# A Griffin-style hybrid layer on one core: value parts behind the squares, queries in large staging tiles, a cast moved, and a softmax scaling on ScalarE

## The chip, the cores and the metric

The kernel runs on one core of a Trainium2 chip. The metric is the device time of one execution in microseconds (us). Before the change three executions took 1650.82, 1650.87 and 1651.36 us; the median is 1650.87 us. The engines of a core run side by side, each through its own queue in order: TensorE (PE) multiplies and transposes, VectorE (DVE) and ScalarE (ACT) read its results from eight accumulator banks (PSUM), GpSimd (POOL) works on the on-chip buffers alone, and SyncE (SP) issues most of the DMA transfers.

## The reference, cut to what matters

One decoder layer with 1024 tokens of width 1024. The normalised input is projected to the inputs of three branches: a sparse attention (A), a convolution (B) and a cross-attention into 256 memory tokens (C). Gates merge them; an output projection and a gated feed-forward block follow. What the change touches:

```python
# A: queries with 8 heads of 64, keys with 2 groups of 64, both RMS-normalised per head
q = rms_norm(heads(q_nsa, NSA_HEADS), nsa_qk_norm[0])
ks = rms_norm(k_s, nsa_qk_norm[2])      # selected keys; vs = v_s
kw = rms_norm(k_w, nsa_qk_norm[3])      # window keys;   vw = v_w
# B: after the convolution, a layer norm over the channels
u = jax.nn.silu(layer_norm(u, conv_ln_g, conv_ln_b))
# C: four heads of 128 into 256 memory tokens
s_m = jnp.einsum('bshd,bmhd->bhsm', qm, km) * (MEM_HEAD_DIM ** -0.5)
p_m = jax.nn.softmax(s_m, axis=-1)
o_m = jnp.einsum('bhsm,bmhd->bshd', p_m, vm)
```

## The kernel before, in words

**Arithmetic.** Products of 32-bit numbers are made of three products of a rounded high part and the remaining low part. `split` (L130) makes the parts: ACT copies the high part (L131), DVE or POOL subtracts it from the source for the low part (L132). `mm3` (L153, matmuls on L146) multiplies.

**The order of the work.** The Python code issues instructions in a program order. A scheduler then orders each engine's queue at compile time by priority, with modelled durations; a buffer pool gives a tile a buffer when one is free, so too few buffers delay an instruction. `follow` (L207) and the manual dependencies add an order without a wait of their own. On the chip each queue then runs in that fixed order and waits wherever an input or a buffer is not ready. Two kinds of work have low priority and fill gaps: the taps of the convolution on DVE (L474, L475; 120 instructions of about 1000 columns) and the merge-gate products on PE (`pf`, in one bank of their own; ACT empties that bank with the copy L1049).

**Stages around the change.** The mixing projections come first, with the convolution's two operands. Then:

- *Memory attention* (L691, about 245 to 366 us of the profiled execution). Eight units, each two heads by 256 tokens: scores on PE, maxima on DVE (L640), exponentials with their sums on ACT (L644), the reciprocal on DVE (L646), then four multiplications of a 128x256 tile by the reciprocal on POOL (L650). DVE turns the probabilities in squares of 32 (L657), SP stores them (L660) and loads them turned (L665). Two units later `mem_out` makes their parts (ACT cast L670, POOL subtractions L673) and multiplies with the values; its outputs are split again (L684) and stored (L686) for a stage after the attention. Between units, `queries` projects one of eight query tiles (evicted by ACT on L344 and L348), whose raw rows go to memory. From the fourth unit on, `square_queries` (L357) loads such a tile back (L361), scales it on POOL (L363), turns it on DVE (L372) and stores it by four DMAs (L376).
- *Key stage* (L727 to L754, about 343 to 412 us). The weights of 512 columns are loaded in four units, three in the weight buffers and the fourth, as high and low tile, in two of the four large tiles (`t4`, 4 KB a partition). For each of eight token tiles, `wide_proj` makes 24 matmuls into one bank; `heads_norm` (L378) squares the keys on ACT (L382), sums on DVE (L384), takes the root on ACT (L138), the reciprocal (L140) and the product (L387) on DVE. Gains (L745), the split of the keys, and the split of the values straight out of the bank (L749) follow; two tiles later PE transposes the keys (L732) and DVE copies them out (L734). Along with the first four tiles run the query tiles 4 to 7 (raw and turned half in two of six small tiles `t2`), and at tiles 1 and 3 the last two memory outputs. These last query tiles are read only by the second half of the sparse attention.
- *Sparse attention* (412 to about 800 us), and the *merge* (to about 940 us), along with which the layer norm over channels runs in steps (`layer_norm`, L1053): two halves of a mean by a product with ones, two of a variance (L1086), each evicted by a root on ACT (L1088). `bank` (L99) gives out the banks of three pools of 3, 2 and 2 buffers in a fixed rotation; `at` names a pool.

Of the kernel before, what the change touches and what calls it, by code (L numbers as in the profile page):

```python
# [8 lines left out]
F32 = mybir.dt.float32  # L9
# [3 lines left out]
OP = mybir.AluOpType  # L13
# [26 lines left out]
def hybrid_layer_kernel(  # L40
# [48 lines left out]
    def t2(shape, dt=F32, p=P):  # L89
        return t2p.tile([p] + shape, dt, tag="t2", name=nm("t2"))  # L90
# [116 lines left out]
    def follow(m, i, why):  # L207
        tc.add_manual_dep(m.ins, i.name, ORDER, reason=why)
# [145 lines left out]
            follow(m, after, "roots behind the exponentials")  # L354
        nc.vector.reciprocal(stat, stat)

    def square_queries(j, t, stat, after=None):  # L357

        h = stat.shape[2]
        raw, sq = t2([512]), t2([512])  # L360
        nc.sync.dma_start(raw, qraw[j, t])  # L361
        v = raw.rearrange("p (h d) -> p h d", h=h)
        m = nc.gpsimd.tensor_tensor(v, v, stat[:, t, :, None].to_broadcast([P, h, 512 // h]), op=OP.mult)  # L363
        if after is not None:
            follow(m, after, "scaled behind the memory values' parts")
        if j == 0:
            nc.vector.transpose(sq.rearrange("p (c h s) -> p h c s", c=4, h=4),
                                raw.rearrange("p (h c s) -> p h c s", h=4, c=4))
            o = qt_m[t].rearrange("c r a x -> r c a x")
        else:  # L370
            for g in range(2):
                nc.vector.transpose(sq.rearrange("p (g c h s) -> p g h c s", g=2, c=2, h=4)[:, g],  # L372
                                    raw.rearrange("p (g h c s) -> p g h c s", g=2, h=4, c=2)[:, g])
            o = qt_n[t].rearrange("g c r a x -> r (g c) a x")
        for a in range(4):
            nc.sync.dma_start(o[:, :, a], sq[32 * a:32 * a + 32].rearrange("p (c x) -> p c x", c=4))  # L376

    def heads_norm(v, qn):  # L378

        a, h, d = v.shape[1:]  # L380
        sq = t2([a, h, d])
        nc.scalar.activation(sq, v, AF.Square)  # L382
        ss = small(a * h)
        nc.vector.tensor_reduce(ss, sq.rearrange("p a h d -> p (a h) d"), axis=AX.X, op=OP.add)  # L384
        r = recip_rms(ss, d, RMS_EPS, a * h)
        rb = r.rearrange("p (a h) -> p a h", a=a)[:, :, :, None].to_broadcast([P, a, h, d])
        nc.vector.tensor_tensor(qn, v, rb, op=OP.mult)  # L387

    def gain_mul(t, g):
        a, h, d = t.shape[1:]  # L390
# [239 lines left out]
    def mem_softmax(hp, tp, QM):  # L630
        pm = t4([2, 2, 256])
        nb, den, rec = small(4), small(4), small(4)
        bs = []
        for tt in range(2):
            b = bank([2, 256])
            bs.append(b)
            for h in range(2):
                mm3(b[:, h, :], QM[:, 0, tt, h].rearrange("p a s -> p (a s)"), QM[:, 1, tt, h].rearrange("p a s -> p (a s)"),
                    KM[:, 0, 2 * hp + h, :], KM[:, 1, 2 * hp + h, :], True, True)
            nc.vector.tensor_reduce(nb[:, 2 * tt:2 * tt + 2], b, axis=AX.X, op=OP.max, negate=True)  # L640
        for tt in range(2):
            for h in range(2):
                j = 2 * tt + h
                exps.append(nc.scalar.activation(pm[:, tt, h, :], bs[tt][:, h, :], AF.Exp, scale=1.0,  # L644
                                                 bias=nb[:, j:j + 1], accum_out=den[:, j:j + 1]).ins)
        nc.vector.reciprocal(rec, den)  # L646
        for tt in range(2):
            for h in range(2):
                j = 2 * tt + h
                nc.gpsimd.tensor_scalar(pm[:, tt, h, :], pm[:, tt, h, :], rec[:, j:j + 1], 1.0,  # L650
                                        op0=OP.mult, op1=OP.mult)
        return pm

    def mem_squares(hp, tp, pm):
# [11 lines left out]
                          pd[hp, tp].rearrange("m c r a x -> (c r) m (a x)"))  # L666
        return PT

    def mem_out(hp, tp, PT):
        follow(nc.scalar.copy(PT[:, 0], PT[:, 1].bitcast(F32)), exps[-1],  # L670
               "parts behind the next unit's exponentials")
        for mb in range(2):
            part = nc.gpsimd.tensor_tensor(PT[:, 1, mb], PT[:, 1, mb].bitcast(F32), PT[:, 0, mb].bitcast(F32),  # L673
                                           op=OP.subtract)
        o = bank([2, 256])
        for hl, h, mb in [(hl, h, mb) for hl in range(2) for h in range(2) for mb in range(2)]:
            hh = 2 * hp + h
            ov = o[:, h, :].rearrange("p (t a s) -> p t a s", t=2, a=4)
            p_ = PT[:, hl, mb, :, h].rearrange("p a t s -> p t a s")
            mm(ov, VM[:, 0, mb, hh * P:(hh + 1) * P], p_, (hl, h, mb) == (0, 0, 0), (hl, h, mb) == (1, 1, 1))  # L680
            if hl == 0:
                mm(ov, VM[:, 1, mb, hh * P:(hh + 1) * P], p_, False, False)
        om = [PT[:, hl, 0].rearrange("p a h t s -> p (a h t s)").rearrange("p (h t) -> p h t", h=2) for hl in range(2)]
        split(om[0], om[1], o)  # L684
        for hl in range(2):
            follow(nc.sync.dma_start(  # L686
                md[2 * hp:2 * hp + 2, :, hl, tp * 256:(tp + 1) * 256].rearrange("h p t -> p h t"),
                om[hl].bitcast(F32)), stored[-1], "outputs behind the squares")
        return part.ins
# [43 lines left out]
        for s in range(2):  # L733
            nc.vector.tensor_copy(key_cols(s, t), b[:, s].bitcast(F32))  # L734

    cats = []
    for t in range(NT):
        if t < 4:
            square_queries(1, 4 + t, rqn)
        v = wide_proj(ws, t).rearrange("p (s a g d) -> p s a g d", s=2, a=2, g=2)  # L740
        if t in (1, 3):
            mem_out(1, 2 + t // 2, rest.pop(0))
        kn = t2([2, 2, 64])
        heads_norm(v[:, :, 0], kn)
        nc.vector.tensor_tensor(kn, kn, gn[:, 2:4, None, :].to_broadcast([P, 2, 2, 64]), op=OP.mult)  # L745
        cat = t2([4, 2, 64], F32R)
        split(cat[:, :, 0, :], cat[:, :, 1, :], kn.rearrange("p s g d -> p (s g) d"))
        for s in range(2):
            split(VSW[s][:, t, :, 0:64], VSW[s][:, t, :, 64:128], v[:, s, 1])  # L749
        cats.append((t, cat))  # L750
        if t > 1:
            keys(*cats.pop(0))
# [300 lines left out]
    def layer_norm(units):  # L1053
# [27 lines left out]
        yield from sum4(0)  # L1081
        for c in halves:
            yield
            pv = bank([512])
            after = products[-1][0]
            follow(mm(pv, ones, U[0][:, 0, c], True, True), after, "means behind the last products")  # L1086
            rs = t2([512])
            nc.scalar.activation(rs, pv, AF.Sqrt, scale=1.0, bias=LN_EPS)  # L1088
            nc.vector.reciprocal(rs, rs)
            yield  # L1090
            for ct in range(4):
                nc.vector.tensor_tensor(U[ct][:, 1, c], U[ct][:, 1, c], rs, op=OP.mult)
                if ct % 2:
                    yield
# [539 lines left out]
```

## Time and profile before

| | |
|---|---|
| median of three runs | 1650.87 us |
| the profiled execution | 1650.37 us |
| its span (first to last instruction) | 1648.7 us |
| PE idle, 270 to 343 us | 3.85 of 73 us |
| PE idle, 343 to 412 us (key stage) | 7.55 of 69 us |
| PE idle, 412 to 850 us | 2.74 of 438 us |
| L650 on POOL | 32 instructions, 25.6 us |
| L363 on POOL, query tiles of the sparse attention | 8 instructions, 11.1 us |
| L670 on ACT | 8 instructions, 8.5 us |

Times within the execution count from the start of the span. A row such as "L650 POOL TENSOR_SCALAR t<-t,sm 128x256 x32" names the line of the kernel, the engine, the operation, what is written and read by the program's tile names, the shape and the count. Tile names are shared: `ps` are the banks of the three pools, `pf` is the bank of the gate products, `fz` its evicted copy, `t` the large and small tiles, `slab` the large buffers, `wsl` and `fsl` the split weights, `st` and `fst` weights as loaded, `sm` small columns. "A <- B" in the waits means that A stood idle until B was done. PE's busy time counts pipelined matmuls whose ends are modelled.

### The profile page before, as it was taken

The page shows a single profiled execution, that of the slowest core. Times are in us where ns is not written, and L with a number is a line of the kernel's source. Part 1 is how long each engine was busy: PE and PEld are TensorE (multiplying, and loading weights), DVE is VectorE, ACT ScalarE, POOL GpSimd, SP SyncE. Part 2 cuts the span into 40 slices and gives each one's busy share as a digit, 9 for nine tenths or more (in the row PEclk, how much of TensorE's full clock was granted, in tenths as well). Part 3 has the DMA queues.
Part 4 walks back from the last instruction along what each step waited for, and adds up shares of the span by engine and source line. Part 5 has one row for each costly group of instructions (what it writes and reads, how often), then busy time and mean ns, then how long its engine had stood idle before and what let it go on. Part 6 is the DMA issues. An engine that isn't in the chain of part 4 may idle for free.

```text
span 1648.7 us, 22758 instructions
## 1 busy us (share of the span) xinstructions
PE 1622.5 (98%) x7952; PEld 1361.7 (83%) x7952; DVE 1100.8 (67%) x1821; ACT 744.2 (45%) x1370; POOL 678.5 (41%) x567
## 2 busy tenths in 40 slices
PE   8999999989999999999999999999999999999999
PEld 6887898777888888888878889888888888888887
DVE  6389989996565665656686868865454554376665
ACT  6311355432776666665565356532322232233332
POOL 2010005850567757664215441465556677300000
PEclk9999999999999999999999999999999999999999
DMA  8544456753365556347754454333334446893763
GB/s 290 181 156 126 142 155 179 225 177 103 119 177 157 170 147 179 117 137 246 258 196 141 179 167 151 110 109 102 109 103 136 157 142 196 306 372 117 234 233 119
DMA packets 254874, 281.03 MB, mean 170 GB/s; under 512 B 24404, under 2 KB 176260, under 8 KB 253222
## 3 DMA queue, kind: packets, MB, share of 16 engines
q1 hardware_dynamic: 247846, 266.98, 50.7%
q10 hardware_dynamic: 6912, 12.59, 2.0%
q8 instruction: 63, 1.03, 0.3%
q14 instruction: 53, 0.43, 0.1%
HBM read 193.52 MB, written 85.98 MB: 170 GB/s over the span
## 4 chain that ended last, share of the span: by engine, by line
PE 80%; DVE 7%; DMA 4%; issue 3%; POOL 2%; ACT 2%; SPq 1%; ACTq 0%; DVEq 0%; POOLq 0%
PE ps L146 43%; PE pf L146 17%; PE ps L1568 11%; PE ps L1336 3%; DVE slab L475 3%; PE ps L974 2%; PE pf L1568 1%; DMA t<-zd 1%; PE ps L238 1%; DMA t<-qraw 1%; DVE slab L132 1%; DMA st<-in_w_in_dram 1%; POOL slab L1148 1%; PE pf L1336 0%; POOL slab L673 0%
## 5 line engine op out<-in xcount | busy, mean ns | idle before, releaser
L146 PE MATMUL ps<-slab,wsl 128*128 128x512 f32 (+2 forms) x1688 | 362.6, 373 | 0.0
L146 PEld LDWEIGHTS ps<-slab,wsl 128*128 128x128 f32 x1688 | 298.3, 188 | 56.7 <-issue 1.4
L146 PE MATMUL pf<-slab,fsl 128*128 128x512 f32 x1236 | 314.6, 396 | 4.4 <-ACT fz L1049 4.4
L146 PEld LDWEIGHTS pf<-slab,fsl 128*128 128x128 f32 x1236 | 227.6, 189 | 48.9 <-ACT fz L1049 6.0
L475 DVE SCALAR_TENSOR_TENSOR slab<-slab,cw 128x1019 f32<-128x1019 f32 (+16 forms) x120 | 167.2, 1398 | 1.3
L1464 DVE TENSOR_TENSOR t<-ps,t 128x512 f32<-128x512 f32 x130 | 88.9, 688 | 112.0 <-PE ps L146 110.8
L146 PE MATMUL ps<-slab,fsl 128*128 128x512 f32 x684 | 161.9, 391 | 0.5 <-ACT slab L1144 0.5
L146 PE MATMUL ps<-slab,slab 128*128 128x512 f32 (+1 forms) x628 | 151.0, 376 | 2.7 <-POOL slab L673 2.6
L146 PEld LDWEIGHTS ps<-slab,fsl 128*128 128x128 f32 x684 | 127.7, 188 | 28.0 <-issue 0.7
L146 PEld LDWEIGHTS ps<-slab,slab 128*128 128x128 f32 x628 | 112.8, 188 | 25.6 <-POOL slab L673 4.2
L1568 PE MATMUL ps<-wsl 128*128 128x512 f32 x495 | 118.9, 389 | 0.0
L1568 PEld LDWEIGHTS ps<-wsl 128*128 128x128 f32 x495 | 92.9, 188 | 19.3
L132 DVE TENSOR_TENSOR wsl<-st,wsl 128x1024 fp32r<-128x1024 f32 x58 | 81.3, 1404 | 29.5 <-ACT wsl L131 27.1
L146 PE MATMUL ps<-wsl,slab 128*128 128x512 f32 (+1 forms) x480 | 96.0, 349 | 2.3 <-DVE wsl L132 1.8
L131 ACT CAST wsl<-st 128x1024 fp32r<-128x1024 f32 x61 | 63.8, 1051 | 71.1 <-PE ps L146 23.9
L146 PE MATMUL ps<-slab,qt 128*128 128x384 f32 (+6 forms) x400 | 93.3, 336 | 0.7 <-DVE sm L837 0.3
L132 DVE TENSOR_TENSOR t<-ps,t 128x512 fp32r<-128x512 f32 (+2 forms) x96 | 61.2, 641 | 40.6 <-ACT t L131 39.7
L146 PEld LDWEIGHTS ps<-wsl,slab 128*128 128x128 f32 x480 | 76.7, 189 | 13.2 <-DVE wsl L132 2.0
L146 PE MATMUL ps<-t,slab 128*128 128x256 f32 (+1 forms) x404 | 86.7, 318 | 0.0
L131 ACT CAST wsl<-t 128x1024 fp32r<-128x1024 f32 x43 | 45.3, 1053 | 87.0 <-POOL t L128 32.7
L1477 POOL TENSOR_TENSOR t<-t,t 128x512 f32<-128x512 f32 x21 | 39.3, 1872 | 109.6 <-DVE t L1464 43.4
L1148 POOL TENSOR_TENSOR slab<-slab,t 128x512 f32<-128x512 f32 x32 | 47.8, 1514 | 81.6 <-DVE t L1147 81.6
(267 smaller groups left out, 2964.2 us busy)
## 6 DMA issues: line engine op xcount, KB each, us to landing
t<-in_w_down_dram SPq DMA_DIRECT2D x70, 256.0 KB, 3.7
fst<-in_w_in_dram SPq DMA_DIRECT2D x24, 512.0 KB, 4.0
zd<-fz ACTq DMA_DIRECT2D x48, 256.0 KB, 2.7
slab<-wd SPq DMA_DIRECT2D x24, 512.0 KB, 4.6
t<-zd SPq DMA_DIRECT2D x24, 512.0 KB, 3.9
st<-in_w_gate_dram SPq DMA_DIRECT2D x22, 512.0 KB, 4.0
st<-in_w_up_dram SPq DMA_DIRECT2D x22, 512.0 KB, 4.2
ad<-t SPq DMA_DIRECT2D x44, 256.0 KB, 2.8
```

The lines of the kernel that those rows point to most:

```text
L131: m = nc.scalar.copy(hi, src)
L132: return m, (eng or nc.vector).tensor_tensor(lo, src, hi.bitcast(F32), op=OP.subtract)
L146: m = nc.tensor.matmul(o, a, b, start=start, stop=stop)
L238: m = nc.tensor.transpose(b[:, kk, tt * P:(tt + 1) * P], js[tt][:, k * P:(k + 1) * P], ident)
L475: return nc.vector.scalar_tensor_tensor(acc[:, s:], u[:, :S - s], cw[:, ct, 30 - s:31 - s], acc[:, s:], op0=OP.mult, op1=OP.add)
L974: nc.tensor.transpose(b[:, j - j0, h, :], tiles[h][:, j * P:(j + 1) * P], ident)
L1148: nc.gpsimd.tensor_tensor(a, a, z, op=OP.add)
L1336: nc.tensor.matmul(B[j], a_(ha, k, j), w[:, hb, k % 2, :], start=start and k == 0 and n_ == 0, stop=stop and k == 3 and n_ == 2, skip_grou ...
L1464: nc.vector.tensor_tensor(o, a_, b_, op=OP.add)
L1477: nc.gpsimd.tensor_tensor(u4, u4, c22, op=OP.mult)
L1568: nc.tensor.matmul(B[t], a_, b_, start=start and k == 0 and j == 0, stop=k == FH - 1 and j == 2, skip_group_check=True)
```

## The change

Five edits:

- `square_fetch` is new and only loads a query tile. In the key stage the tiles 4 and 5 are fetched ahead of the loop, 6 and 7 behind the first two uses, each into one large tile whose halves hold the raw and the turned rows.
- `heads_norm` takes two callbacks. In the key stage the high parts of the values (two ACT copies) come directly behind the squares, and the low parts (two DVE subtractions) directly behind the sum, in place of the split at the end of a tile's work. It returns the squares' instruction.
- The last memory output's cast (`mem_out` at tile 3) is ordered behind the squares of key tile 1 and not behind the last exponential.
- The four multiplications of a memory unit by the reciprocals go from POOL to ACT, as copies with a scale.
- The second variance product of the layer norm takes its bank from the first pool; the rotation moves on as before.

```diff
-    def square_queries(j, t, stat, after=None):
+    def square_fetch(j, t, bufs):
+        nc.sync.dma_start(bufs[0], qraw[j, t])
+        return bufs
+
+    def square_queries(j, t, stat, after=None, bufs=None):
 
         h = stat.shape[2]
-        raw, sq = t2([512]), t2([512])
-        nc.sync.dma_start(raw, qraw[j, t])
+        raw, sq = bufs or square_fetch(j, t, (t2([512]), t2([512])))
...
-    def heads_norm(v, qn):
+    def heads_norm(v, qn, highs=None, others=None):
 
         a, h, d = v.shape[1:]
         sq = t2([a, h, d])
-        nc.scalar.activation(sq, v, AF.Square)
+        m = nc.scalar.activation(sq, v, AF.Square)
+        if highs:
+            highs()
         ss = small(a * h)
         nc.vector.tensor_reduce(ss, sq.rearrange("p a h d -> p (a h) d"), axis=AX.X, op=OP.add)
+        if others:
+            others()
         r = recip_rms(ss, d, RMS_EPS, a * h)
         rb = r.rearrange("p (a h) -> p a h", a=a)[:, :, :, None].to_broadcast([P, a, h, d])
         nc.vector.tensor_tensor(qn, v, rb, op=OP.mult)
+        return m.ins
...
-                nc.gpsimd.tensor_scalar(pm[:, tt, h, :], pm[:, tt, h, :], rec[:, j:j + 1], 1.0,
-                                        op0=OP.mult, op1=OP.mult)
+                nc.scalar.activation(pm[:, tt, h, :], pm[:, tt, h, :], AF.Copy, scale=rec[:, j:j + 1])
...
-    def mem_out(hp, tp, PT):
-        follow(nc.scalar.copy(PT[:, 0], PT[:, 1].bitcast(F32)), exps[-1],
+    def mem_out(hp, tp, PT, after=None):
+        follow(nc.scalar.copy(PT[:, 0], PT[:, 1].bitcast(F32)), after or exps[-1],
                "parts behind the next unit's exponentials")
...
-    cats = []
+    def fetch(t):
+        r = t4([2, 512])
+        return square_fetch(1, t, (r[:, 0], r[:, 1]))
+
+    cats, fetched, kept = [], [fetch(4), fetch(5)], []
     for t in range(NT):
         if t < 4:
-            square_queries(1, 4 + t, rqn)
+            square_queries(1, 4 + t, rqn, bufs=fetched.pop(0))
+            if t < 2:
+                fetched.append(fetch(6 + t))
         v = wide_proj(ws, t).rearrange("p (s a g d) -> p s a g d", s=2, a=2, g=2)
         if t in (1, 3):
-            mem_out(1, 2 + t // 2, rest.pop(0))
+            mem_out(1, 2 + t // 2, rest.pop(0), kept[t - 2] if t == 3 else None)
         kn = t2([2, 2, 64])
-        heads_norm(v[:, :, 0], kn)
+        vh, vl = ([VSW[s][:, t, :, 64 * l:64 * l + 64] for s in range(2)] for l in range(2))
+
+        def highs():
+            for s in range(2):
+                nc.scalar.copy(vh[s], v[:, s, 1])
+
+        def others():
+            for s in range(2):
+                sub(nc.vector, vl[s], v[:, s, 1], vh[s].bitcast(F32))
+
+        kept.append(heads_norm(v[:, :, 0], kn, highs, others))
         nc.vector.tensor_tensor(kn, kn, gn[:, 2:4, None, :].to_broadcast([P, 2, 2, 64]), op=OP.mult)
         cat = t2([4, 2, 64], F32R)
         split(cat[:, :, 0, :], cat[:, :, 1, :], kn.rearrange("p s g d -> p (s g) d"))
-        for s in range(2):
-            split(VSW[s][:, t, :, 0:64], VSW[s][:, t, :, 64:128], v[:, s, 1])
         cats.append((t, cat))
...
+            turn[1] += c is halves[1]
-            pv = bank([512])
+            pv = bank([512], at=0 if c is halves[1] else None)
             after = products[-1][0]
```

## The prediction

> **What bounds the kernel now.** I read the page first, then the busy times by stage, then who makes TensorE (PE) wait, and last the chain of work inside the stage that the change edits.
>
> ```profile
> span 1648.7 us, 22758 instructions
> PE 1622.5 (98%) x7952; PEld 1361.7 (83%) x7952; DVE 1100.8 (67%) x1821; ACT 744.2 (45%) x1370; POOL 678.5 (41%) x567
> ```
>
> PE is busy 1622.5 of 1648.7 us. The change adds no matmul and takes none away, so whatever it is worth lies in the 26 us in which PE stands still, or runs slowly. The busy times by stage say where those are (columns: window, its length, then busy time and count for PE, PEld, DVE, ACT and POOL, the granted clock, DMA share, GB/s).
>
> ```profile
> 270.00:343.00 73.00, 69.15 (x356) 57.41 (x355) 71.06 (x78) 39.84 (x94) 54.59 (x47) 1.00 0.77 226
> 343.00:412.00 69.00, 61.45 (x289) 50.46 (x288) 52.14 (x105) 17.85 (x51) 15.92 (x12) 0.98 0.38 116
> 412.00:850.00 438.00, 435.26 (x2323) 371.31 (x2322) 271.80 (x826) 289.31 (x651) 250.95 (x258) 1.00 0.56 175
> ```
>
> The end of the memory attention (270 to 343) leaves PE idle for 3.9 us, the key stage (343 to 412) for 7.5 us, and the whole attention behind it, 438 us long, for 2.7 us. In the first DVE is full (71.06 of 73 us, with the convolution taps of L475 as its cheap filling); in the second nothing is full, so its idle time is waiting. Who is waited for:
>
> ```profile
> PE pf L146 <- ACT fz L1049: 4.4, 5, 2.9
> PE ps L146 <- POOL slab L673: 2.6, 3, 1.3
> PE ps L732 <- DVE t L132: 2.0, 1, 2.0
> PE ps L146 <- DVE wsl L132: 1.8, 1, 1.8
> PE ps L146 <- ACT t L131: 1.2, 2, 1.0
> PE ps L146 <- ACT t L1088: 0.5, 1, 0.5
> ```
>
> The columns are total, times, longest. The 2.9 us, the 2.0 us and the 1.8 us are single events of the key stage. The chain of waits shows the first:
>
> ```profile
> 384.32 2.77 DMA t<-qraw
> 387.25 1.05 POOL t L363
> 388.33 0.77 DVE t L372 x2
> 389.10 0.31 DVE sm L384
> 389.43 0.21 ACT sm L138
> 389.64 0.48 ACT fz L1049
> 390.17 6.48 PE pf L146 x21
> ```
>
> A query tile that only the later attention needs is loaded (L361), scaled on POOL (L363) and turned on DVE (L372). DVE runs its queue in order, so the key statistics (L384) stand behind L372; ACT's root (L138) stands behind those; and the copy L1049, which empties the one bank of the gate products, stands behind the root. PE, which would have filled its time with gate products, waits for that bank. The load came so late because it stood on SP behind the previous tile's stores (L376). The second wait has a chain too:
>
> ```profile
> 359.93 1.05 ACT slab L670
> 360.98 0.29 ACT t L382
> 361.30 0.42 DVE sm L384
> 361.71 1.70 DVE slab L475
> 365.54 0.41 DVE t L387
> 365.95 1.62 DVE slab L475
> 367.57 0.33 DVE t L745
> 368.11 1.16 DVE slab L475
> 369.27 0.07 DVE t L132
> ```
>
> ACT held the squares of the first key tile (L382) behind the last memory cast (L670), which was waiting for its load; then each DVE step of the tile's normalisation stood behind a tap.
>
> **The 2.9 us cost more than themselves.** The same windows around that gap:
>
> ```profile
> 387.20:390.10 2.90, 0.07 (x1) 0.00 (x0) 1.47 (x5) 0.67 (x3) 1.04 (x1) 0.95 0.03 9
> 390.10:393.30 3.20, 3.13 (x8) 2.50 (x9) 3.17 (x8) 1.98 (x6) 0.00 (x0) 0.51 0.51 155
> ```
>
> Behind the gap PE was granted 0.51 of its clock for 3.2 us: 3.2 x (1 - 0.51) = 1.6 us of work lost. A 2.9 us gap is enough for that here. The Trainium skill ("TensorE: Matmul & The Clock Gate", Part 1) puts the fall to half clock after an idle window of about 3.4 us and gives as a rule that no gap may pass that; by it this gap would not be charged, and the sum below would be 5.2 us and not 6.8, the time 1645.7. The row decides, and gives that no chance: the clock did fall.
>
> **The change, part by part.**
>
> *Queries in large tiles.* The loads of query tiles 4 and 5 leave SP at the start of the key stage, those of 6 and 7 after tiles 4 and 5, each into a buffer of the four-buffer pool of large tiles (4 KB a partition, raw half and turned half) and no longer into two of the six small ones. The number of loads, scalings, turns and stores is the same; four issues move ahead of stores on SP.
>
> ```profile
> L361 SPq DMA_DIRECT2D t<-qraw x16: 323/455/1117, 88.0 to 384.3; - x16
> ```
>
> At 455 ns each (median) that is 1.8 us of SP earlier and 1.8 us less later, net nothing. DVE then finds L372's input there, L384 is not held, L1049 comes at once: the 2.9 us and the 1.6 us of half clock go. This I count in full, 4.5 us. Only if the tiles are not free in time does it not come (a rival below). What is late next on that place is the copy of the single gate bank itself, a fraction of a microsecond.
>
> *Last cast later.* L670 of the last memory unit is now ordered behind the squares of the second key tile. The first tile's squares then don't wait for a load. The cast (1.05 us), its two subtractions (L673), the 12 products and the stores behind them come later; nobody reads these stores before the end of the attention, hundreds of microseconds on, so the delay costs nothing. The chain above then starts earlier by at least the cast's own 1.05 us.
>
> *Value parts directly behind squares.* In the trace:
>
> ```profile
> ACT slab L131 <- DVE t L387: 11.6, 7, 4.0
> ```
>
> The value casts wait for L387, because one bank's readers are kept in program order across engines. Now the two casts follow the squares on ACT, and the two subtractions run on DVE between the sum and the reciprocal, while ACT takes the root. A bank is free after L387 and not after four more steps. The key chain gets two short casts (128x128; less than the 0.41 us below) before the root and two subtractions before L140, at most 0.8 us on each engine, and about 0 where ACT and DVE wait for each other anyway. With the earlier start, of the 2.0 us wait at L732 I take 1.5 as gained; the ends are 2.0 gained, and 1.8 lost (next to the taps, below).
>
> *Scaling on ACT.* POOL's 32 multiplications become 32 ACT copies with a scale.
>
> ```profile
> L650 POOL TENSOR_SCALAR t<-t,sm 128x256 f32<-128x256 f32 x32 | 25.6, 816 | 1.2 <-DVE sm L646 1.2
> L650 POOL TENSOR_SCALAR t<-t,sm x32: 472/482/2478, 251.8 to 349.9; 128x256 f32<-128x256 f32 x32
> L131 ACT CAST t<-t 128x256 fp32r<-128x256 f32 x10 | 3.6, 414 | 0.0
> ```
>
> POOL loses 25.6 us; ACT gains some 32 x 0.414 = 13.2 us (the nearest row, the same shape between buffers) in a stretch where it was busy 39.84 of 73 us. A unit's four take 1.7 us in place of 3.3, and the subtractions L673 and L132 no longer stand behind them on POOL. Of the 2.6 us that PE waits for L673 I take 0.8 as gained (ends: 0, if it is the casts L670 ahead of POOL that are late, and 2.6). DVE gains hardly anything:
>
> ```profile
> 343.61 2.02 DVE L475 SCALAR_TENSOR_TENSOR slab<-slab,cw 128x1008 f32<-128x1008 f32 x1
> 347.26 1.24 DVE L475 SCALAR_TENSOR_TENSOR slab<-slab,cw 128x1007 f32<-128x1007 f32 x1
> 344.53 2.00 POOL L363 TENSOR_TENSOR t<-t,spent 128x512 f32<-128x512 f32 x1
> 346.52 3.84 POOL L650 TENSOR_SCALAR t<-t,sm 128x256 f32<-128x256 f32 x4
> ```
>
> A tap beside POOL's L363 takes 2.02 us, one beside L650 takes 1.24: it is L650 that gets stretched (482 ns median, 2478 longest), not the tap. The Trainium skill ("SBUF — State Buffer", SBUF: two separate sides) calls the port pair of DVE and POOL an exclusive lock, held for a whole instruction; by it each L650 could hold off a tap for its 0.48 us, 32 x 0.48 = 15 us of DVE freed as an estimate from the row. The two taps speak against any such size, so I count 0; the case in which it comes is a rival.
>
> The cost is ACT's order. The four copies wait for the reciprocal L646, and that stands among the taps:
>
> ```profile
> 335.24 0.20 ACT L644 ACTIVATION_READ_ACCUMULATOR t<-ps,sm 128x1 f32 x1
> 341.12 0.17 DVE L646 RECIPROCAL sm<-sm 128x4 f32<-128x4 f32 x1
> ```
>
> In the last unit 5.7 us lie between the last exponential and its reciprocal. POOL could wait that long at no cost; ACT has behind it the copies that empty PE's banks (L344, L1049) and weight casts. The cost lies between 0 (the compile-time order puts these ahead of the scaling) and 5.7 us plus a half clock for a unit like the last. I take 1.0 in all: most of what ACT does then does not feed PE at once.
>
> *Layer norm bank.* The second variance product takes a bank of the first pool; the 0.5 us wait for L1088 should go: 0.5.
>
> *Key weights.* The 1.8 us wait for the weights' subtraction (DVE wsl L132) is not edited. POOL and DVE arrive a little earlier; I take 0.5 (ends 0 and 1.8).
>
> **The sum.** 2.9 + 1.6 + 1.5 + 0.8 + 0.5 + 0.5 - 1.0 = 6.8 us. The profiled execution took 1650.37 us (its span 1648.7 and 1.7 around it) and lies 0.5 us under the median 1650.87: 1650.87 - 6.8 = 1644.1 us.
>
> **The rivals.**
>
> *Everything relaxes.* With POOL freed, and DVE too, the memory stage's waits go (L673 1.8 more, the casts' 1.2), the weights' 1.3 more, L732's last 0.5, and ACT costs nothing (1.0): 6.8 + 5.8 = 12.6, 1638.3 us. For it speaks DVE at 71.06 of 73 us; against it the tap that took 1.24 us. (The lock that the Trainium skill describes in "SBUF — State Buffer" would be a way to it.) Chance 0.14.
>
> *The taps take the stage back.* PE arrives earlier at the key transposes, by the 4.5 us, but each step of the chain still stands behind a tap (1.70, 1.62 and 1.16 us above). Then L732's wait is not 0.5 but 2.0 + 1.8, and weights and POOL give nothing: 6.8 - 3.3 - 0.5 - 0.8 = 2.2, 1648.7 us. For it: taps are not touched. Against: they sit early in the stage. Chance 0.14.
>
> *The change does not do what it says.* The large pool's four buffers also hold the last memory unit and the last quarter of the key weights. If the fetches wait for these, tiles 6 and 7 arrive late again and 4.5 us stay: 1648.6 us. Against it: two buffers free themselves before the stage needs them, and query tile 6 is used two key tiles later. Chance 0.08.
>
> *Slower: ACT is blocked by the scaling.* Place: the eight units of the memory attention. If two of them stall PE as long as the last reciprocal lags, each also falls to half clock: 2 x (5.7 + 1.6) = 14.6, less the 7.8 of the gains: 1657.7 us. It decides against the change from 11.1 us of stalls on (7.8 + 3.3). Against it: ACT was idle for 33 of 73 us. Chance 0.08.
>
> **How the numbers follow.** The forecast gets 0.56. A difference of 0.2% (3.3 us) is about what a measurement of this kernel can tell from no change, so faster means under 1647.6. Forecast and first rival lie there: 0.70; the two that end at 1648.7 make no change: 0.22; slower 0.08. The range runs from 1639.0, just above the first rival, to 1650.5, above both of the unchanged ones; it leaves out the slower case and the tail of the first rival. The likeliest case alone spans 1641.5 to 1647.
>
> **What would show it.** Right: in the changed profile no PE wait for L1049 over 1 us between 343 and 412, no stretch there at a clock of 0.5, no DVE wait of L372 for L363, L382 of the first key tile no longer behind L670, L650 on ACT at about 0.41 us each, and no wait for L1088. The memory stage's idle 3.9 us should shrink slightly and the attention's 2.7 us stay. Wrong: a wait of PE for ACT between 270 and 343 that was not there, a half clock anywhere new, or L732's wait grown. If the key stage loses its 4.5 us and the time still stays, the static order of the fillers gave it back after 412.

## The result and the profile after

The changed kernel takes 1642.59 us (median of four runs, 1641.7 to 1643.48), the kernel before beside it 1651.11 us (1650.82 to 1653.25): a ratio of 0.9948, 95% interval 0.9937 to 0.9960, 8.5 us less. The forecast was 1644.1 us and 6.8 us less. The sum is near; what stands in it is not, as the profile after and twelve more kernels show.

The page of the profiled execution (1642.26 us) begins:

```profile
span 1640.2 us, 22729 instructions
PE 1621.2 (99%) x7952; PEld 1363.5 (83%) x7952; DVE 1095.1 (67%) x1821; ACT 756.0 (46%) x1402; POOL 658.3 (40%) x535
```

POOL is 20 us less busy and ACT 12 us more. By stages, the columns as before:

```profile
270.00:343.00 73.00, 71.54 (x380) 61.16 (x379) 72.01 (x85) 52.37 (x122) 46.66 (x28) 1.00 0.81 243
343.00:412.00 69.00, 64.10 (x295) 52.47 (x294) 47.15 (x107) 16.34 (x50) 10.33 (x8) 0.95 0.30 95
412.00:850.00 438.00, 436.40 (x2320) 371.87 (x2319) 275.44 (x819) 290.21 (x650) 249.74 (x257) 1.00 0.56 175
```

Read the counts before the busy time. In the 73 us of the memory stage PE began 380 matmuls, not 356. Its busy time rose by only 2.4 us, but 24 matmuls at 71.54 / 380 = 0.188 us are 4.5 us of work; by their shapes, twelve of 512 columns at 0.227 us and twelve of 256 at 0.118 us (median distance between two starts), 4.1 us. So busy time also holds some longer distances between matmuls. In the key stage PE is idle for 4.9 us in place of 7.5, but its mean clock fell from 0.98 to 0.95. From 412 to 850 the idle time fell from 2.7 to 1.6 us. One stretch further on, before and then after:

```profile
850.00:1060.00 210.00, 209.17 (x1041) 176.47 (x1040) 162.89 (x198) 108.25 (x163) 82.69 (x51) 1.00 0.44 147
```

```profile
850.00:1060.00 210.00, 210.00 (x1050) 178.53 (x1049) 162.44 (x200) 106.93 (x162) 92.18 (x55) 1.00 0.45 151
```

The last 0.8 us of idle time are gone there. By these counts the changed kernel is 24 matmuls ahead at 343 us, 30 at 412 us, 27 at 850 us and 36 at 1060 us. Who PE waits for, in the changed kernel (fz L1049 has become L1070, POOL L673 is L680, L732 is L739, the last cast L670 is L677; a wait of 6.0 us near the start, 5.9 before, is left out):

```profile
...
PE ps L146 <- ACT slab L677: 3.4, 1, 3.4
PE pf L146 <- ACT fz L1070: 1.0, 3, 0.4
PE ps L146 <- DVE t L132: 1.0, 2, 0.6
PE ps L146 <- POOL slab L680: 0.8, 2, 0.4
...
PE ps L739 <- DVE t L132: 0.5, 1, 0.5
```

The single 2.9 us for fz and the 1.8 us for the key weights are gone, and the 2.0 us at the key transposes have become 0.5. In their place stands a wait that was not there, 3.4 us for the last memory cast, at 359.2 us. The windows around it:

```profile
359.20:362.60 3.40, 0.01 (x1) 0.00 (x0) 2.47 (x5) 1.95 (x5) 1.29 (x1) 1.00 0.39 116
362.60:369.50 6.90, 6.38 (x21) 5.10 (x22) 6.90 (x12) 0.68 (x2) 3.33 (x2) 0.53 0.24 76
```

Behind it PE has 0.53 of its clock for 6.9 us: 6.9 x 0.47 = 3.2 us lost, twice the 1.6 us of before. So the wait and the half clock behind it cost 6.6 us, where the fz gap and its half clock had cost 4.5. What PE waited for is in DVE's queue:

```profile
350.16 0.77 DVE L375 STREAM_TRANSPOSE t<-t 128x256 f32<-128x256 f32 x2 [2.94 <-POOL t L366]
350.85 1.40 DVE L483 SCALAR_TENSOR_TENSOR slab<-slab,cw 128x1005 f32<-128x1005 f32 x1
352.18 0.76 DVE L375 STREAM_TRANSPOSE t<-t 128x256 f32<-128x256 f32 x2
352.86 1.22 DVE L483 SCALAR_TENSOR_TENSOR slab<-slab,cw 128x1004 f32<-128x1004 f32 x1
354.00 0.41 DVE L389 TENSOR_REDUCE sm<-t 128x4 f32<-128x256 f32 x1
...
360.17 0.42 DVE L768 TENSOR_TENSOR t<-t,spent 128x256 f32<-128x256 f32 x1
```

and in ACT's:

```profile
360.63 0.41 ACT L131 CAST t<-t 128x256 fp32r<-128x256 f32 x1 [5.98 <-DVE t L768]
360.94 0.38 ACT L385 ACTIVATE t<-ps 128x256 f32<-128x256 f32 x1
361.21 0.42 ACT L761 CAST slab<-ps 128x128 fp32r<-128x128 f32 x2
361.51 1.07 ACT L677 CAST slab<-slab 128x1024 fp32r<-128x1024 f32 x1
```

DVE stands 2.94 us before the turn of a query tile (L375), whose rows have just been fetched and scaled. Behind it come a tap, a second query tile, a tap, and only then the sum of the first key tile (L389, 354.00). The root on ACT follows, then reciprocal, product and gains on DVE, each of these three behind a tap and the last also behind the turns of a third query tile (358.34). Then ACT can cast that tile's keys (360.63), and the squares of the second tile and the last memory cast, which the change put behind those squares, follow. PE had finished the products of four key tiles and the fillers that fit by 359.2.

The first row maximum of the sparse attention (one row of the trace, first and last start; before, then after) tells how far ahead the kernel is:

```profile
L848 DVE DVE_READ_ACCUMULATOR2_ANT sm<- x208: 73/83/85, 417.0 to 779.8; 128x1 f32 x104
```

```profile
L869 DVE DVE_READ_ACCUMULATOR2_ANT sm<- x208: 72/83/89, 411.1 to 773.1; 128x1 f32 x104
```

It begins 5.9 us earlier and ends 6.7 us earlier, and the span is 8.5 us shorter. Two thirds of the lead in matmuls (24 of 36) are there before the key stage begins. Does it come from the scaling, or from the key stage's edits, as the prediction's terms have it?

### The profile page after: what moved, and what is told of

Same layout as the page of the kernel before. It is cut to its first block, busy times and chain, and to the rows that moved or that the text cites. A ratio compares the mean times of both kernels' runs of the same rounds, so it can differ in the third digit from the quotient of the medians.

```text
span 1640.2 us, 22729 instructions
## 1 busy us (share of the span) xinstructions
PE 1621.2 (99%) x7952; PEld 1363.5 (83%) x7952; DVE 1095.1 (67%) x1821; ACT 756.0 (46%) x1402; POOL 658.3 (40%) x535
## 4 chain that ended last, share of the span: by engine, by line
PE 83%; DVE 8%; POOL 2%; DMA 2%; issue 2%; ACT 1%; SPq 1%; ACTq 0%; DVEq 0%; POOLq 0%
PE ps L146 47%; PE pf L146 16%; PE ps L1590 11%; PE ps L1358 4%; DVE slab L483 4%; PE ps L995 2%; PE pf L1590 1%; PE ps L238 1%; DMA t<-qraw 1%; PE pf L1358 1%; POOL slab L797 1%; POOL slab L132 0%; POOL wsl L797 0%; DVE wsl L132 0%; SPq L379 0%
## 5 line engine op out<-in xcount | busy, mean ns | idle before, releaser
L483 DVE SCALAR_TENSOR_TENSOR slab<-slab,cw 128x1019 f32<-128x1019 f32 (+16 forms) x120 | 160.4, 1341 | 1.3
L131 ACT CAST wsl<-st 128x1024 fp32r<-128x1024 f32 x61 | 63.9, 1052 | 72.0 <-PE ps L146 24.6
L131 ACT CAST wsl<-t 128x1024 fp32r<-128x1024 f32 x43 | 45.3, 1053 | 87.9 <-POOL t L128 33.5
```

Of the source, the lines that this page charges most:

```text
L131: m = nc.scalar.copy(hi, src)
L483: return nc.vector.scalar_tensor_tensor(acc[:, s:], u[:, :S - s], cw[:, ct, 30 - s:31 - s], acc[:, s:], op0=OP.mult, op1=OP.add)
```

## The experiments

My theory after the first look gave the scaling 2.4 us, the fall of the memory stage's idle time from 3.85 to 1.46 us. The rival gave it nothing and the whole gain to the key stage, as the prediction had. Each kernel was timed beside the kernel before (medians 1651.76, 1650.70 and 1650.97 us in the three sessions). The ratios are estimated over the single executions and not from the two medians; they differ by up to 0.001 from the medians' quotient.

| kernel | median us | ratio to before | 95% interval |
|---|---|---|---|
| u_scale: change, scaling back on POOL | 1649.0 | 0.9989 | 0.9980 to 0.9998 |
| o_scale: before, scaling on ACT alone | 1641.82 | 0.9949 | 0.9936 to 0.9961 |
| o_scale_pool: the same, POOL loaded again | 1645.13 | 0.9962 | 0.9949 to 0.9976 |
| o_dve: before, scaling on DVE | 1651.87 | 1.0003 | 0.9994 to 1.0012 |
| u_cast: change, last cast ordered as before | 1642.56 | 0.9948 | 0.9936 to 0.9961 |
| u_values: change, values split at the end | 1643.79 | 0.9961 | 0.9949 to 0.9974 |
| u_tiles: change, queries in small tiles | 1639.38 | 0.9926 | 0.9913 to 0.9939 |
| c_prod_late: change, last memory products later | 1641.88 | 0.9944 | 0.9930 to 0.9957 |
| q_later: change, query tiles two key tiles later | 1641.93 | 0.9946 | 0.9933 to 0.9958 |
| q_follow: q_later, turns behind the first keys | 1634.58 | 0.9900 | 0.9884 to 0.9916 |
| c_taps: change without the last 14 taps (its output lacks them) | 1641.28 | 0.9940 | 0.9926 to 0.9953 |
| o_scale_qfollow: o_scale, turns behind the first keys | 1641.17 | 0.9936 | 0.9923 to 0.9949 |

### Which half of the change brings the time

u_scale is the change without the edit of the scaling, o_scale that edit alone.

```diff
# u_scale, on the changed kernel
-                nc.scalar.activation(pm[:, tt, h, :], pm[:, tt, h, :], AF.Copy, scale=rec[:, j:j + 1])
+                nc.gpsimd.tensor_scalar(pm[:, tt, h, :], pm[:, tt, h, :], rec[:, j:j + 1], 1.0, op0=OP.mult, op1=OP.mult)
# o_scale, on the kernel before: the same two lines the other way round, and nothing else
```

> The change with the four multiplications of a memory unit back on POOL, all else as changed. Theory A (the scaling on ACT is what took PE's idle time between 270 and 343 us from 3.85 to 1.46 us): about 2.4 us slower than the change, 1645 us, with the idle time of that stage back near 3.9 us. Rival B (the whole gain is made in the key stage; the scaling only moves work between engines): within 1 us of the change, 1642.6 us.

> The kernel before with the scaling on ACT alone. Theory A: the memory stage's idle time falls by some 2.4 us and the key stage keeps its 7.5 us: 1648.5 us. Rival B: 1651 us, no change. Rival C (ACT blocked by the reciprocal's wait): slower than 1652 us, with PE waits for ACT between 250 and 343 us.

All forecasts missed both kernels: u_scale is 4 us slower than the slower one had it, and o_scale 6.7 us faster than the fastest. o_scale alone is as fast as the whole change (0.9949 and 0.9948); everything but the scaling is worth 1.8 us (u_scale, 0.9989, interval 0.9980 to 0.9998). The prediction had given the scaling 0.8 - 1.0 = -0.2 us, and the key stage's edits 6.0. In u_scale PE's waits of the key stage are no smaller than before:

```profile
PE ps L146 <- ACT slab L678: 4.2, 1, 4.2
PE ps L146 <- DVE wsl L132: 2.7, 1, 2.7
```

### Why the scaling is worth it

Two mechanisms were open: POOL's queue is freed (its subtractions come earlier), or the softmax chain is shorter on ACT. o_scale_pool loads POOL with a multiplication of the same shape for every copy, whose result nobody reads; o_dve frees POOL without touching ACT.

```diff
# o_scale_pool, on o_scale
                 nc.scalar.activation(pm[:, tt, h, :], pm[:, tt, h, :], AF.Copy, scale=rec[:, j:j + 1])
+                nc.gpsimd.tensor_scalar(spent[:, 256:512], spent[:, 0:256], rec[:, j:j + 1], 1.0,
+                                        op0=OP.mult, op1=OP.mult)
# o_dve, on the kernel before
-                nc.gpsimd.tensor_scalar(pm[:, tt, h, :], pm[:, tt, h, :], rec[:, j:j + 1], 1.0,
+                nc.vector.tensor_scalar(pm[:, tt, h, :], pm[:, tt, h, :], rec[:, j:j + 1], 1.0,
```

> The kernel before with the scaling on ACT, and beside each of the 32 copies a POOL multiplication of the same shape that also waits for the reciprocal and writes into constants no longer in use, so that POOL keeps the 25.6 us that it was rid of. Theory A (the gain of the scaling is POOL's queue: its parts for L132 and L673 stand no longer behind the scaling): most of the 9 us goes again, 1648 to 1650 us. Rival B (the gain is the shorter chain from exponentials to turned squares, four scalings in 1.7 us for 3.3): the gain stays, 1642 to 1644 us. Rival C (DVE gains, because POOL takes less of the port pair that they share): the taps' mean, 1.40 us before, stays there and the gain goes as under A.

> The kernel before with the four multiplications on DVE in place of POOL, and nothing on ACT. Theory A (POOL's queue): POOL is rid of them, most of the gain comes, less what DVE, which is full there, pays for 32 more instructions: 1643 to 1647 us. Rival B (the shorter chain): DVE does them in its own queue right before it turns the squares, the chain is as short: also 1643 to 1647 us. Rival C (DVE's time is what bounds the memory stage): 32 more instructions of about 0.3 us make it slower than ACT's by 10 us: 1651 us or more.

The whole memory stage (245 to 343 us), in the order before, o_scale, o_scale_pool, o_dve:

```profile
245.00:343.00 98.00, 94.15 (x494) 79.23 (x493) 94.68 (x103) 50.68 (x122) 65.96 (x59) 1.00 0.71 209
```

```profile
245.00:343.00 98.00, 96.36 (x518) 82.92 (x517) 94.56 (x111) 66.83 (x159) 52.07 (x32) 1.00 0.75 227
```

```profile
245.00:343.00 98.00, 94.27 (x500) 80.36 (x500) 92.22 (x103) 62.38 (x152) 69.38 (x58) 1.00 0.70 210
```

```profile
245.00:343.00 98.00, 93.49 (x486) 79.61 (x486) 97.84 (x125) 46.97 (x117) 37.14 (x27) 0.98 0.64 189
```

How long ACT waits there for the score maxima on DVE (total, times, longest), in the same order:

```profile
ACT t L644 <- DVE sm L640: 29.5, 11, 6.6
```

```profile
ACT t L644 <- DVE sm L640: 9.5, 7, 3.3
```

```profile
ACT t L644 <- DVE sm L640: 9.9, 5, 3.8
```

```profile
ACT t L644 <- DVE sm L640: 24.5, 10, 6.4
```

And the taps there, before and in o_scale:

```profile
L475 DVE SCALAR_TENSOR_TENSOR slab<-slab,cw 128x1013 f32<-128x1013 f32 (+29 forms) x35 | 55.2, 1581 | 0.1
```

```profile
L475 DVE SCALAR_TENSOR_TENSOR slab<-slab,cw 128x1013 f32<-128x1013 f32 (+29 forms) x36 | 50.9, 1417 | 0.1
```

With the scaling on ACT, DVE does the same taps in less time (mean 1581 to 1417 ns, 36 x 0.164 = 5.9 us of a full engine), the maxima come earlier, and PE fits 24 more matmuls into the same 98 us. Loading POOL again (69.38 us busy) leaves ACT's wait short (9.9 us), but takes 18 of the 24 matmuls back, and 2 us of the time by the ratios (3.3 us by the medians); the two intervals overlap. The time, 1645.13 us, lies between what the queue alone (1648 to 1650) and the shorter chain alone (1642 to 1644) would give. So more than half of the gain (6.3 of 8.4 us by the ratios) is there with POOL as loaded as before, and part of it may be POOL's queue: the matmuls say so, the times do not tell it apart from nothing. Freeing POOL at DVE's expense brings nothing at all: DVE is busy for 97.84 of 98 us. My expectation for o_dve had the multiplication's cost on DVE wrong:

```profile
L650 DVE TENSOR_SCALAR t<-t,sm x28: 341/824/1390, 251.7 to 336.3; 128x256 f32<-128x256 f32 x28
```

Its median in this stage is 824 ns (584 ns over all 32), where 300 had been assumed.

POOL's total load does not order the taps: they took 1474 ns on the mean in o_scale_pool, with POOL at its fullest. What POOL does meanwhile does, when the 35 taps that begin between 245 and 343 us are sorted by it (from the traces' starts and ends; POOL's are rough). In the kernel before, 8 taps beside no POOL instruction took 1.25 us on the mean, 3 beside multiplications alone 1.33, and 18 beside two-input instructions alone (the subtractions and L363) 1.78, the longest 2.32. In o_scale_pool these means are 1.26 (7 taps), 1.37 (9) and 1.67 (15). So a tap is long mainly beside a two-input instruction, and hardly beside a multiplication. In o_scale 24 taps ran beside two-input instructions, at 1.51 us; why they are stretched less there is not shown. Nor do shorter taps alone explain the short wait of ACT: in o_dve they took 1357 ns, the least of the four, and the wait is 24.5 us.

### The key stage's edits one by one

```diff
# u_cast, on the changed kernel
-            mem_out(1, 2 + t // 2, rest.pop(0), kept[t - 2] if t == 3 else None)
+            mem_out(1, 2 + t // 2, rest.pop(0))
# u_values
-        kept.append(heads_norm(v[:, :, 0], kn, highs, others))
+        kept.append(heads_norm(v[:, :, 0], kn))
...
+        for s in range(2):
+            split(VSW[s][:, t, :, 0:64], VSW[s][:, t, :, 64:128], v[:, s, 1])
# u_tiles
-            square_queries(1, 4 + t, rqn, bufs=fetched.pop(0))
-            if t < 2:
-                fetched.append(fetch(6 + t))
+            square_queries(1, 4 + t, rqn)
```

> The change with the last memory cast ordered behind the last exponential again, as before. Theory A (the new order is itself what PE waits for: a gap of 3.4 us for the cast L677, and behind it 6.8 us at half clock, another 3.4 us): the gap goes, about 5 us faster than the change, 1637.5 us. Rival B (the gap comes from the query loads that hold DVE up, and the new order spares the first tile's squares a wait): 1 to 3 us slower than the change, 1644 to 1645.5 us.

> The change with the values split at the end of a tile's work again, as before. Theory A (the new order frees a bank some steps earlier, but the first tile's chain behind DVE's queue is what is late): within 1 us of the change, 1642.6 us. Rival B (the earlier free bank is worth the 1.5 us that the prediction gave it with the cast): 1644 us or more.

> The change without its large staging tiles: the queries are fetched at each key tile's turn into small tiles again. If the early fetches are worth nothing (theory: VectorE waited for the fetched rows in the changed kernel too, 4.6 us against 6.5 before), this is within 1.5 us of the change, ratio 0.994 to 0.9955, with the gap of 3 to 4 us before 365 us still there. If the prediction's step was right (the large tiles bring the rows early enough to shorten the first tile's chain), the gap and the half clock behind it grow and it is 2.5 us or more slower than the change, ratio over 0.996.

The place of the last cast is worth nothing (0.9948 twice), which neither forecast had: with the old order the cast is done early, and the same gap ends at the key transposes instead (3.5 us). The value parts may be worth 1 to 2 us (0.9961, intervals overlapping); their profiled execution also had half clock in stages that the edit does not touch, so I read no more from it. The large tiles look like a loss (the intervals only touch, at 0.9937 to 0.9939), and the trace shows why. Without them PE's wait before the first key transposes is

```profile
PE ps L739 <- DVE t L132: 1.9, 1, 1.9
```

in place of 3.4 us, the key stage's clock 0.98 in place of 0.95, and the time 3.2 us less. Both theories had it no faster than the change. The early fetches did bring the rows earlier, for two tiles at once, and so in the changed kernel the turns of all four tiles stand ahead of the first key tile's last subtraction (363.36). With small tiles only the first query tile's do (351.21). The first sum comes no earlier there (354.35, behind a second tap in place of the second tile), but the steps behind it are not held, and the last subtraction is at 361.01.

### What makes the gap of 3.4 us

Three answers: the order on PE (the last memory products are planned too early), the turns of the query tiles ahead of the first key sum, or the taps between the steps of the first key chain.

```diff
# c_prod_late, on the changed kernel: in mem_out, for the last memory output; behind = the last key product of tile 3
+            m = mm(ov, VM[:, 0, mb, hh * P:(hh + 1) * P], p_, (hl, h, mb) == (0, 0, 0), (hl, h, mb) == (1, 1, 1))
+            if behind is not None:
+                follow(m, behind, "outputs behind the last key products")
# q_later, on the changed kernel
-        if t < 4:
-            square_queries(1, 4 + t, rqn, bufs=fetched.pop(0))
-            if t < 2:
-                fetched.append(fetch(6 + t))
+        if 2 <= t < 6:
+            square_queries(1, 2 + t, rqn, bufs=fetched.pop(0))
+            if t < 4:
+                fetched.append(fetch(4 + t))
# q_follow, on q_later: for each of a query tile's turns
+                if behind is not None:
+                    follow(m, behind, "turned behind the first keys")
# with behind = the last subtraction of the first key tile's split
# c_taps, on the changed kernel; NOUT = 14
-            while j < len(taps) and run * (len(taps) + TAP_LEAD) >= j * total:
+            while j < len(taps) - NOUT and run * (len(taps) + TAP_LEAD) >= j * total:
# o_scale_qfollow: o_scale with the edits of q_later (small tiles) and q_follow
```

> The change, and the products of the last memory output ordered on PE behind the key products of tile 3. Theory A (PE stands at the cast only because its queue has these 12 products too early): the 3.4 us gap and the 3.4 us lost to half clock go, 1636 to 1637 us. Rival B (what is late is the DVE work that waits for query loads; PE would stand at the key transposes in place of the products): 1641.5 to 1643 us.

> The change with the query tiles 4 to 7 handled at key tiles 2 to 5 and not 0 to 3. Theory A (PE's 3.4 us gap in the key stage comes from DVE, whose queue holds the first key tile's sum, L389, behind query transposes that wait for POOL and for the late loads): the gap and the half clock behind it go, some 5 to 6 us, 1637 us. Rival B (the taps between the steps of that chain are enough to keep it late): the gap stays at 2 us or more, 1640.5 to 1643 us.

Both times lie where the rivals put them, but not for the rivals' reasons. The products that c_prod_late was to hold back stood behind the key tiles' products already, and its wait is 3.8 us for the same cast. q_later moved the query tiles in the program, but that only changes a priority: the scheduler gave the turns the same place on DVE, at 350.07 us with a wait of 3.18. So neither tested what it was to test.

> The change, with the turns of the fetched queries (VectorE, two instructions of 0.77 us a tile) put behind the first key tile's last subtraction; nothing else is moved. In the changed kernel VectorE stood 2.94 us before these turns, for the fetched rows, and the first tile's sum came behind two tiles of them, at 354.00 us. Theory (the gap of 3.4 us of TensorE at 362 us is the length of the first key tile's chain on VectorE): the sum now comes at about 350 us, the chain ends about 5 us earlier, the gap is under 0.7 us and the granted clock stays full between 343 and 412 us: 5 to 7 us less than the change, about 1636 us, ratio 0.991. Rival (the taps between the steps, or ScalarE's queue, hold the chain; the turns only fill a hole): a gap of 2 us or more stays, with half clock behind it, and the time is within 1.5 us of the change (0.9945 to 0.995).

> The change without the last 14 taps of the convolution (of 124; its output lacks them): those that VectorE did between 344 and 375 us as filler between the steps of the first key tiles. The turns of the fetched queries stay ahead of the first sum. Theory (length of the first tile's chain): the sum waits for the turns as before, until about 351.7 us, but the five taps behind it (5 x 1.25 = 6.2 us) are gone from the chain: gap under 0.7 us, full clock, 5 to 7 us less than the change, ratio about 0.991. Rival (the wait for the fetched rows alone holds the chain, taps only fill holes): the gap stays at 2 us or more and the time within 1.5 us of the change. If both this kernel and the one with the turns behind lose the gap, neither alone is its cause: the sum of both is.

> The kernel before with two edits alone: the scaling of the memory probabilities on ScalarE, and the query turns behind the first key tile's last subtraction (their place in the program two tiles later). No split of the value parts, no large tiles, no bank of its own. Theory (the change's own key edits are worth nothing, the turns are what holds the key stage): as fast as the change with the turns behind, about 1636 us, ratio 0.991, gap of TensorE under 1 us. Rival (the change's key edits do their part once the turns are out of the way): 3 us or more slower than that one, a wait of 2 us or more left between 343 and 412 us.

q_follow has the order forced; it keeps q_later's places in the program as well. DVE's queue there:

```profile
349.33 0.41 DVE L391 TENSOR_REDUCE sm<-t 128x4 f32<-128x256 f32 x1
...
354.76 0.41 DVE L770 TENSOR_TENSOR t<-t,spent 128x256 f32<-128x256 f32 x1
355.10 1.25 DVE L485 SCALAR_TENSOR_TENSOR slab<-slab,cw 128x1000 f32<-128x1000 f32 x1
356.27 0.41 DVE L132 TENSOR_TENSOR t<-t,t 128x256 fp32r<-128x256 f32 x1
356.60 1.41 DVE L375 STREAM_TRANSPOSE t<-t 128x256 f32<-128x256 f32 x4
```

The first sum is at 349.33 in place of 354.00, the gains at 354.76 in place of 360.17. The gap is gone, and so is the half clock:

```profile
343.00:412.00 69.00, 67.95 (x331) 56.32 (x330) 52.96 (x134) 23.91 (x78) 16.09 (x17) 1.00 0.36 110
```

```profile
L871 DVE DVE_READ_ACCUMULATOR2_ANT sm<- x208: 74/83/88, 403.2 to 765.3; 128x1 f32 x104
```

The attention begins 7.9 us earlier than in the changed kernel, and the median is 8.0 us lower: 1634.58 us, ratio 0.9900 (0.9884 to 0.9916), the fastest of all. Against q_later, which differs in this order alone, it shows that the turns of the query tiles, ahead of the first key sum and between the steps behind it, made the gap with these taps in place.

The taps' part is not settled. Without them the first chain ends early too, as the theory had it (last subtraction at 354.99 us, with the turns still ahead of the sum), and the wait for the cast is gone, but others come (columns total, times, longest):

```profile
PE ps L147 <- POOL slab L681: 2.3, 2, 1.4
PE ps L740 <- DVE t L133: 0.9, 1, 0.9
```

The shorter queue was planned anew. PE has the first key transposes early, then waits 2.3 us for the last memory output's subtractions on POOL, which stand there behind the scaling of a query tile, and 0.9 us at the next key transposes: 3.2 us in all, mean clock 0.98, and a time (0.9940) that can't be told from the change. What the taps cost in this chain stays open.

o_scale_qfollow says what the change's other edits are for. With the same turns held back it is no faster than o_scale (0.9936 and 0.9949, intervals overlapping) and 6.6 us slower than q_follow. Its wait:

```profile
PE ps L146 <- DVE slab L735: 3.3, 2, 2.8
```

PE stands 2.8 us for a copy of key columns that is queued on DVE behind the second tile's product and gains; a half clock follows (0.98). So the rival was right here: two edits are not enough, and with the turns out of the way the change's other key edits do their part. Which of them does was not tried apart.

## Why the prediction was right in sum and wrong in its parts

- *Scaling on ACT*, predicted +0.8 - 1.0: this is the step that failed most. Alone it brings 8.4 us (1 - 0.9949 of 1651). The prediction said "DVE gains hardly anything", from one tap of 2.02 us and one of 1.24; over the 35 taps of the stage the mean fell by 0.164 us. As to the multiplications its reading of the two taps holds (1.33 us beside them, 1.25 beside nothing), but the taps got shorter all the same. It looked for the gain in PE's idle time (3.85 us in 73), and the stage gave 24 matmuls, 4.1 to 4.5 us of work, of which 2.4 had been idle time and the rest spacing inside busy time. Of the terms, POOL's came larger than predicted (L673's 2.6 us became 0.8, so 1.8 and not 0.8 was gained). The ACT cost of 1.0 was hardly seen: between 270 and 343 the only new wait of PE for ACT is 0.3 us for a weight cast that had waited for its load, and the 1.2 us for ACT's cast L131 are gone.
- *The price of a scaling*, 0.414 us by the nearest cast and 13.2 us for 32:

```profile
L658 ACT ACTIVATE t<-t,sm x32: 492/513/536, 251.8 to 333.5; 128x256 f32<-128x256 f32 x32
```

  The median is 0.513 us, but four in a row take 1.71 us, the 1.7 of the prediction, because they overlap: 13.7 us for all 32, near the 13.2. The Trainium skill ("ScalarE: Activation LUTs", Rules for kernel authors) gives about 0.3 us and 0.83 ns per element for an activation whose bias is a column operand; here the column is the scale, an estimate of 0.3 + 256 x 0.00083 = 0.51 us, and the trace agrees. The same table tells to put a multiplication on VectorE, not ScalarE, for its speed per element in bf16; here, with 32-bit data, o_dve (1.0003) against o_scale (0.9949) says the opposite: DVE was busy for 97.84 of 98 us.
- *Queries in large tiles*, 2.9 + 1.6 counted "in full": the wait for fz did go (longest 0.4 us), but it is gone without the large tiles too (0.4 in u_tiles, 0.7 in o_scale), so it is not theirs alone. And "what is late next on that place" was not the gate bank, it was the first key chain. 3.4 us of gap and 3.2 us of half clock replaced 2.9 and 1.6. L375 still waits for POOL, for 4.6 us in total where L372 waited for 6.5. Against small tiles the large ones cost about 3 us.
- *Last cast later*: the first tile's squares do come at once (L385 at 347.69 us, L382 at 360.89 before), but with the old order, in u_cast, they come at 348.78, so the edit moved them by 1.1 us. It is worth nothing, since the sum behind them was held on DVE.
- *Value parts*, 1.5: L739's wait fell from 2.0 to 0.5, as predicted, but it is 0.5 in u_values too, without this edit; against u_values the time fell by 1 to 2 us, not told apart from nothing. With the turns held back they, or the other edits beside them, count.
- *Key weights*, 0.5: the wait of 1.8 us is gone in the changed kernel, and in u_scale it is 2.7 us. It came with the scaling.
- *Layer norm bank*, 0.5: the wait for L1088 is gone and the 0.8 us of idle time between 850 and 1060. All nine kernels with the edit, u_scale among them, are busy there for 210.00 us. Of the five without it only o_scale is; the others have 209.17 (before), 208.92 (o_dve), 208.94 (o_scale_pool) and 209.13 (o_scale_qfollow). So this term came about as predicted, and not with the scaling; the edit was not tried alone.

By idle time and clock: memory stage 3.85 to 1.46, key stage 7.55 to 4.90, attention 2.74 to 1.60, then 0.83 to 0, together 7.0 us; 1.6 us more lost to half clock; and 4.5 - 2.4 = 2.1 us of closer matmuls (1.7 by their shapes). That is 7.0 - 1.6 + 2.1 = 7.5 of the span's 8.5 us; 1.0 us (1.4) I have not placed.

Two of the rivals came true in part, each in its own stage: the memory stage relaxed, and the key stage was taken back by DVE's queue, though by turns of query tiles and not only by the taps that the rival named. One of the prediction's own signs of being wrong, a half clock anywhere new, is there at 363 us. That the sum was near is luck: one error of some 8 us and one of some 6, with opposite signs, made a good number.

## What to carry to other kernels

Read a stage by how many matmuls it gets done and not by its idle time: where another engine is full, PE's busy time can already hold part of the loss. When a gap is removed, follow the in-order queue of the engine behind it to the next consumer, and ask what is planned ahead of that; an early fetch lets a side job in ahead of the chain that matters. If a side job must stand behind a chain, order it there by a dependency: a later place in the program did not move it.

## What the hardware did that I had not expected

- Half clock followed PE's gaps in pieces of 3.4 us: one piece behind the 2.9 us before and behind 3.6 us in o_scale (stage mean 0.98), two behind the 3.4 us of the changed kernel (6.9 us at 0.53). The length of the gap alone does not decide: one piece followed a gap of 1.9 us in u_tiles, and none followed one of 2.7 us in u_scale (at 347.4 us; clock 1.00 in the 3.4 us behind it). The Trainium skill ("TensorE: Matmul & The Clock Gate", HAM oscillation — how this bites in real kernels) names gaps over about 3.4 us as the rule; here 2.9 was enough, and once 1.9.
- The same multiplication of 128x256 took 472 to 2478 ns on POOL (kernel before, median 482), 337 to 1390 ns on DVE (o_dve, median 584) and 492 to 536 ns on ACT (changed kernel, median 513). In the memory stage the means on POOL and DVE were alike, 793 and 817 ns. Only on ACT did it hardly vary.
